# Row sums on one core: a body with its own semaphores behind an empty tile context, and no barrier at the end

## The chip, the cores and the metric

The kernel runs on one core of a Trainium2 chip. A core has five engines with instruction streams of their own: PE (TensorE, not used here), DVE (VectorE), ACT (ScalarE), POOL (GpSimd) and SP (SyncE, which issues transfers), and 16 DMA engines that work off the transfers. Engines and transfers order themselves by semaphores only. The metric is the device time of one execution in microseconds (us), as the median of several executions. Lower is better.

## The reference

```python
x = np.random.randn(32, 512, 1024).astype(np.float32)   # batch, seq, dim

def reference(x):
    return np.sum(x, axis=-1).astype(np.float32)
```

16384 rows of 1024 float32 are each added up to one number: 67.1 MB are read and 64 KB written.

## The kernel before

The rows are laid over the 128 partitions in two blocks. In the first block, 14336 rows, every partition has 112 rows of its own, in the second, 2048 rows, 16. A buffer (`xt`) holds 16 rows of every partition, 8 MB, and there are three of them (`bufs=3`, line 36).

**Loads.** SP issues all loads, in one queue. The loop of lines 84 to 99 runs over the seven buffers of the first block; each is loaded by two transfers, the even and the odd partitions (line 93). For the first buffer a small transfer with one row of every partition comes ahead of the two. A buffer can be loaded anew only when its sums are done. The second block comes in five pieces: 9, 4 and 2 rows into a buffer (line 107), and its last row in two parts of 544 and 480 columns into `tail` (line 110). Lines 145 to 164 move the first three loads to the start of the program, ahead of the barrier that the program begins with (its instructions are at line 178 of the profile).

**Sums.** DVE adds up whole buffers with one `tensor_reduce` each (line 47). Of the seventh buffer ACT takes seven rows (line 55, an `activation` with an accumulator, one row at a time). When the first block is done, ACT issues the store of its results in three transfers, the early stores (line 116). Of the pieces of 9 and 4 rows DVE takes 4 and 2, ACT 5 and 2; of the piece of 2 rows DVE takes the first, with an operation that adds the two halves of a row pairwise and accumulates (`pairs_dve`, line 67), and ACT the second. The last row is two pairwise sums on DVE: the first leaves its partial sum in a column of `tail`, and the second reads it back among its own inputs. Line 128 is a copy of two columns of `tail` between the two; nothing reads what it writes.

**Order.** The body is traced in a tile context, which gives each engine's instructions in program order and works out the semaphores: an increment behind an operation that another waits for, and waits attached to instructions, or in instructions of their own where there are several. Transfers use eight semaphores in turn, so that a ninth waits for the first. Line 132 puts SP's wait for ACT's last row in front of the last store (line 133).

**The end.** `tc.close()` and `tc.compile()` (lines 140 and 141) end the context: SP waits for every transfer, all engines meet in a barrier, POOL clears the context's semaphores, and all engines meet in a second barrier. In the profile these instructions stand at line 141.

Of the kernel before, what the change touches and what calls it, by code (L numbers as in the profile page):

```python
# [1 line left out]

# [4 lines left out]

F32 = mybir.dt.float32
ADD = mybir.AluOpType.add
COPY = mybir.ActivationFunctionType.Copy  # L10
X = mybir.AxisListType.X

BLOCKS = (112, 16)
G = 16
ACT_ROWS = 7
CUT = 544
EARLY = 3


@with_exitstack  # L20
def row_sums(
    ctx: ExitStack,
    tc: tile.TileContext,
    x: bass.AP,
    out: bass.AP,
):
    nc = tc.nc
    P = nc.NUM_PARTITIONS

    x_flat = x.flatten_outer_dims()  # L30
    R, D = x_flat.shape
    C = R // P
    assert R % P == 0 and sum(BLOCKS) == C
    out_flat = out.rearrange("a (b c) -> (a b c)", c=1)

    xpool = ctx.enter_context(tc.tile_pool(name="x", bufs=3))
    rpool = ctx.enter_context(tc.tile_pool(name="res", bufs=1))


    tail = rpool.tile([P, D + 16], F32, name="tail")  # L40
    part = tail[:, CUT + 14 : CUT + 15]
    nc.vector.memset(tail[:, CUT + 15 : CUT + 16], 0.0)  # L42
    seen = rpool.tile([P, 2], F32, name="seen")
    pairs = [rpool.tile([P, D // 2], F32, name=f"pairs{i}") for i in range(3)]

    def rows_dve(xt, res, j, n, c):
        nc.vector.tensor_reduce(  # L47
            out=res[:, c : c + n],
            in_=xt[:, j * D : (j + n) * D].rearrange("p (j d) -> p j d", d=D),
            axis=X,  # L50
            op=ADD,
        )

    def sum_act(v, acc):
        return nc.scalar.activation(out=v, in_=v, func=COPY, accum_out=acc)  # L55

    by_act = []

    def rows_act(xt, res, j, n, c):
        for i in range(n):  # L60
            by_act.append(
                sum_act(xt[:, (j + i) * D : (j + i + 1) * D], res[:, c + i : c + i + 1])
            )

    def pairs_dve(v, a, b, acc, pairs):
        h = (a + b) // 2
        nc.vector.tensor_tensor_reduce(  # L67
            out=pairs[:, 0 : h - a], in0=v[:, a:h], in1=v[:, h:b], scale=1.0, scalar=0.0,
            op0=ADD, op1=ADD, accum_out=acc,
        )  # L70

    def block(r0, n):
        x_b = x_flat[r0 : r0 + P * n].rearrange("(p c) d -> p (c d)", p=P)
        out_b = out_flat[r0 : r0 + P * n].rearrange("(p c) -> p c", p=P)
        return x_b, out_b, rpool.tile([P, n], F32, name=f"res{r0}")

    full = C - G
    done = 0
    for b, n in enumerate(BLOCKS):
        x_b, out_b, res = block(done * P, n)  # L80
        final = b == len(BLOCKS) - 1
        whole = n - G if final else n
        c = 0
        while c < whole:
            m = min(G, whole - c)
            xt = xpool.tile([P, G * D], F32, tag="xt", name="xt")


            parts = [(q, 0, m) for q in (slice(0, P, 2), slice(1, P, 2))]
            if done + c == 0:  # L90
                parts = [(slice(0, P), 0, 1)] + [(q, 1, m) for q, i, k in parts]
            for q, i, k in parts:
                nc.sync.dma_start(  # L93
                    out=xt[q, i * D : k * D], in_=x_b[q, (c + i) * D : (c + k) * D]
                )
            a = ACT_ROWS if done + c + m == full else 0
            rows_dve(xt, res, 0, m - a, c)
            rows_act(xt, res, m - a, a, c + m - a)
            c += m
        if not final:  # L100
            out_a, res_a = out_b, res
        done += n

    xt = xpool.tile([P, G * D], F32, tag="xt", name="xt")
    cuts = [0, 9, 13, 15]
    for i, k in zip(cuts, cuts[1:]):
        nc.sync.dma_start(out=xt[:, i * D : k * D], in_=x_b[:, (c + i) * D : (c + k) * D])
    last = 15 * D
    for i, k, gap in ((0, CUT, 0), (CUT, D, 16)):
        nc.sync.dma_start(  # L110
            out=tail[:, i + gap : k + gap],
            in_=x_b[:, c * D + last + i : c * D + last + k],
        )

    for i, k in ((0, 104), (104, 116), (116, P)):
        nc.scalar.dma_start(out=out_a[i:k], in_=res_a[i:k])

    by_act.clear()
    for i, k in zip(cuts[:2], cuts[1:3]):
        h = (k - i) // 2  # L120
        rows_dve(xt, res, i, h, c + i)
        rows_act(xt, res, i + h, k - i - h, c + i + h)
    pairs_dve(xt, 13 * D, 14 * D, res[:, c + 13 : c + 14], pairs[2])
    rows_act(xt, res, 14, 1, c + 14)
    pairs_dve(tail, 0, CUT, part, pairs[0])


    nc.vector.tensor_copy(out=seen, in_=tail[:, CUT + 14 : CUT + 16])  # L128
    pairs_dve(tail, CUT + 14, D + 16, res[:, c + 15 : c + 16], pairs[1])


    tc.keep_in_program_order(nc.sync.keepalive_nop([nc.sync.lower_ap(res[:, c + 14 : c + 15])]))
    store = nc.sync.dma_start(out=out_b, in_=res)
    for i in by_act:
        tc.declare_no_dep(store.ins, i.ins, reason="the wait is in the nop before it")


def kernel(tc: tile.TileContext, x: bass.AP, out: bass.AP):
    row_sums(tc, x, out)
    tc.close()  # L140
    tc.compile()  # L141

    sp = mybir.EngineType.SP
    fn = tc.nc.m.functions[0]
    entry, body = None, None
    for blk in fn.blocks:
        ops = [i for i in blk.instructions if i.engine == sp]
        if entry is None:  # L150
            entry = blk
        elif any(i.opcode == "DMACopy" for i in ops):
            body = blk
            break
    code = list(body.instructions)
    loads = [i for i in code if i.engine == sp][:EARLY]
    for load in loads:
        assert load.opcode == "DMACopy" and not load.sync_info.on_wait
        code.remove(load)
    body.instructions = code  # L160
    code = list(entry.instructions)
    at = next(k for k, i in enumerate(code) if i.engine == sp and i.opcode == "Drain")
    code[at:at] = loads
    entry.instructions = code

# [1 line left out]
_INS = ['x']  # L167
_OUTS = [((32, 512), 'float32')]


# [23 lines left out]
```

## Time and profile before

| | us |
|---|---|
| time, median of 3 runs (161.99 to 162.24) | 162.09 |
| profiled execution: span, first to last instruction | 160.28 |
| profiled execution: first instruction to the last semaphore event behind the span | 162.19 |
| DVE busy | 121.5 (76%) |
| ACT busy | 17.1 (11%) |
| DMA, mean over the span | 419 GB/s |

The span is what the profile shows of one execution; behind it the trace records only semaphore events, for another 1.91 us. The page names engines with a q (SPq, DVEq) for instructions of the engine's sequencer, such as waits, drains and the issue of transfers. They don't count as busy. A transfer has two times: when it is issued, and when it has landed, which is when the last of the 16 increments of its semaphore comes.

### The profile page before, as it was taken

The page shows a single profiled execution, that of the slowest core. Times are in us where ns is not written, and L with a number is a line of the kernel's source. Part 1 is how long each engine was busy: PE and PEld are TensorE (multiplying, and loading weights), DVE is VectorE, ACT ScalarE, POOL GpSimd, SP SyncE. Part 2 cuts the span into 40 slices and gives each one's busy share as a digit, 9 for nine tenths or more (in the row PEclk, how much of TensorE's full clock was granted, in tenths as well). Part 3 has the DMA queues.
Part 4 walks back from the last instruction along what each step waited for, and adds up shares of the span by engine and source line. Part 5 has one row for each costly group of instructions (what it writes and reads, how often), then busy time and mean ns, then how long its engine had stood idle before and what let it go on. Part 6 is the DMA issues. An engine that isn't in the chain of part 4 may idle for free.

```text
span 160.3 us, 138 instructions
## 1 busy us (share of the span) xinstructions
DVE 121.5 (76%) x17; ACT 17.1 (11%) x31; POOL 0.2 (0%) x4
## 2 busy tenths in 40 slices
DVE  0000059997699968999499994999949999599884
ACT  0000000000000000000000000000000000596694
POOL 0000000000000000000000000000000000000000
DMA  9979996996996996996997998979969969998991
GB/s 376 491 337 399 491 523 262 523 523 262 523 507 278 523 491 294 523 491 294 523 474 311 523 409 376 523 343 442 523 278 507 523 262 523 432 432 370 402 407 66
DMA packets 2293, 67.18 MB, mean 419 GB/s; under 512 B 629, under 2 KB 757, under 8 KB 1013
## 3 DMA queue, kind: packets, MB, share of 16 engines
q1 hardware_dynamic: 2128, 67.12, 97.4%
q10 hardware_dynamic: 165, 0.06, 0.1%
HBM read 67.11 MB, written 0.07 MB: 419 GB/s over the span
## 4 chain that ended last, share of the span: by engine, by line
DMA 73%; DVE 23%; another core or an unknown queue 1%; SPq 1%; issue 0%; DVEq 0%
DMA xt<-in_x_dram 73%; DVE res L47 21%; DVE pairs L67 1%; SPq L93 1%; DVE seen L128 0%; DVEq L47 0%; DVE tail L67 0%; DVE res L67 0%; DVEq L141 0%
## 5 line engine op out<-in xcount | busy, mean ns | idle before, releaser
L47 DVE TENSOR_REDUCE res<-xt 128x16 f32<-128x16384 f32 (+3 forms) x9 | 119.8, 13309 | 34.0 <-DMA xt<-in_x_dram 34.0
L55 ACT ACT_TABLE_LOAD x1 | 1.3, 1283 | 138.2 <-DMA xt<-in_x_dram 138.2
L55 ACT ACTIVATE xt<-xt 128x1024 f32<-128x1024 f32 x15 | 15.6, 1043 | 2.6 <-DMA out_dram<-res 2.6
L55 ACT ACTIVATION_READ_ACCUMULATOR xt<-xt 128x1 f32 x15 | 2.8, 187 | 0.0
L42 DVE MEMSET tail<- 128x1 f32 x1 | 0.1, 59 | 2.3 <-PEq L178 2.3
L67 DVE CUSTOM_DVE_ANT_0 pairs<-tail 128x272 f32<-128x272 f32 (+1 forms) x2 | 0.9, 426 | 0.0
L67 DVE CUSTOM_DVE_ANT_0 pairs<-xt 128x512 f32<-128x512 f32 x1 | 0.7, 692 | 0.2 <-DMA xt<-in_x_dram 0.2
L128 DVE COPY seen<-tail 128x2 f32<-128x2 f32 x1 | 0.2, 170 | 0.0
L67 DVE DVE_READ_ACCUMULATOR2_ANT res<- 128x1 f32 x2 | 0.2, 82 | 0.0
L178 POOL MEMSET const-bfloat16-1.0<- 128x1 bf16 x1 | 0.1, 102 | 0.0
L178 POOL MEMSET const-uint8-127<- 128x1 uint8 x1 | 0.1, 101 | 0.0
L178 POOL MEMSET const-float32-0.0<- 128x1 f32 x1 | 0.1, 99 | 0.2 <-issue 0.2
L178 POOL MEMSET const-float32-1.0<- 128x1 f32 x1 | 0.1, 98 | 0.0
L67 DVE DVE_READ_ACCUMULATOR2_ANT tail<- 128x1 f32 x1 | 0.1, 83 | 0.0
## 6 DMA issues: line engine op xcount, KB each, us to landing
xt<-in_x_dram SPq DMA_DIRECT2D x2, 3840.0 KB
xt<-in_x_dram SPq DMA_DIRECT2D x1, 4608.0 KB, 32.3
xt<-in_x_dram SPq DMA_DIRECT2D x1, 2048.0 KB, 36.8
xt<-in_x_dram SPq DMA_DIRECT2D x1, 1024.0 KB, 37.7
xt<-in_x_dram SPq DMA_DIRECT2D x1, 512.0 KB
tail<-in_x_dram SPq DMA_DIRECT2D x1, 272.0 KB, 28.6
tail<-in_x_dram SPq DMA_DIRECT2D x1, 240.0 KB, 19.5
xt<-in_x_dram SPq DMA_DIRECT2D x12, 38.5
```

What stands on the lines that cost most here:

```text
L42: nc.vector.memset(tail[:, CUT + 15 : CUT + 16], 0.0)
L47: nc.vector.tensor_reduce(out=res[:, c : c + n], in_=xt[:, j * D : (j + n) * D].rearrange("p (j d) -> p j d", d=D), axis=X, op=ADD,)
L55: return nc.scalar.activation(out=v, in_=v, func=COPY, accum_out=acc)
L67: nc.vector.tensor_tensor_reduce(out=pairs[:, 0 : h - a], in0=v[:, a:h], in1=v[:, h:b], scale=1.0, scalar=0.0, op0=ADD, op1=ADD, accum_out ...
L93: nc.sync.dma_start(out=xt[q, i * D : k * D], in_=x_b[q, (c + i) * D : (c + k) * D])
L128: nc.vector.tensor_copy(out=seen, in_=tail[:, CUT + 14 : CUT + 16])
L178: nc = _bacc.Bacc("TRN2", target_bir_lowering=False, num_devices=1)
```

## The change

The body is no longer traced in the tile context. The context is closed and compiled while it is empty, and the body is written behind it with waits and increments by hand. The three buffers, `tail` and the results are allocated directly. These are the edits:

- Each buffer has one semaphore for both halves (32 per round), each piece one of its own; DVE and ACT count their operations in `vec` and `act`.
- SP waits for a buffer's sum (`vec`) ahead of its next load and for nothing else; the waits for old transfers are gone, and the last five loads follow each other.
- The copy at line 128 is gone; the second sum of the last row waits for DVE's own count instead.
- In front of the last store SP waits for `vec` and for `act`.
- At the end SP waits for the early stores, clears all semaphores but one, and waits for the last store. No engine meets another.
- The first three loads are moved to the start of the program as before.

```diff
-    nc.vector.tensor_copy(out=seen, in_=tail[:, CUT + 14 : CUT + 16])
-    pairs_dve(tail, CUT + 14, D + 16, res[:, c + 15 : c + 16], pairs[1])
-    tc.keep_in_program_order(nc.sync.keepalive_nop([nc.sync.lower_ap(res[:, c + 14 : c + 15])]))
-    store = nc.sync.dma_start(out=out_b, in_=res)
-    for i in by_act:
-        tc.declare_no_dep(store.ins, i.ins, reason="the wait is in the nop before it")
...
+    nc.vector.wait_ge(sems["first"], 16)
+    for b in range(n_bufs):
+        a = ACT_ROWS if b == n_bufs - 1 else 0
+        nc.vector.wait_ge(slots[b % BUFS], 32 * (b // BUFS + 1))
+        rows_dve(xt[b % BUFS], 0, G - a, res_a, b * G)
+        freed[b] = count["vec"]
+        if a:
+            nc.scalar.wait_ge(slots[b % BUFS], 32 * (b // BUFS + 1))
+            rows_act(xt[b % BUFS], G - a, a, res_a, b * G + G - a)
+    body_vec, body_act = count["vec"], count["act"]
+    nc.scalar.wait_ge(vec, body_vec)
+    nc.scalar.wait_ge(act, body_act)
     for i, k in ((0, 104), (104, 116), (116, P)):
-        nc.scalar.dma_start(out=out_a[i:k], in_=res_a[i:k])
+        nc.scalar.dma_start(out=out_a[i:k], in_=res_a[i:k]).then_inc(sems["early_store"], 16)
+    for k in range(2):
+        i, j = CUTS[k], CUTS[k + 1]
+        h = (j - i) // 2
+        nc.vector.wait_ge(sems[f"piece{k}"], 16)
+        rows_dve(last, i, h, res_z, i)
+        nc.scalar.wait_ge(sems[f"piece{k}"], 16)
+        rows_act(last, i + h, j - i - h, res_z, i + h)
+    nc.scalar.wait_ge(sems["piece2"], 16)
+    rows_act(last, 14, 1, res_z, 14)
+    nc.vector.wait_ge(sems["piece2"], 16)
+    pairs_dve(last, 13 * D, 14 * D, res_z[:, 13:14], pairs[2])
+    nc.vector.wait_ge(sems["tail0"], 16)
+    pairs_dve(tail, 0, CUT, tail[:, CUT + 14 : CUT + 15], pairs[0])
+    nc.vector.wait_ge(sems["tail1"], 16)
+    nc.vector.wait_ge(vec, count["vec"])
+    pairs_dve(tail, CUT + 14, D + 16, res_z[:, 15:16], pairs[1])
...
+    for b, dst, src, s in loads:
+        if b >= BUFS:
+            nc.sync.wait_ge(vec, freed[b - BUFS])
+        nc.sync.dma_start(out=dst, in_=src).then_inc(s, 16)
+    nc.sync.wait_ge(vec, count["vec"])
+    nc.sync.wait_ge(act, count["act"])
+    nc.sync.dma_start(out=out_z, in_=res_z[:, :]).then_inc(sems["store"], 16)
+    nc.sync.wait_ge(sems["early_store"], 48)
+    nc.sync.sem_clear(range(numbers[0], sems["store"].num))
+    nc.sync.wait_ge(sems["store"], 16).then_inc(sems["store"], -16)
...
 def tile_reduce_tiled_1024_kernel(tc: tile.TileContext, x: bass.AP, out: bass.AP):
-    row_sums(tc, x, out)
     tc.close()
     tc.compile()
+    nc = tc.nc
+    row_sums(nc, x, out)
```

## The prediction

> **What bounds the kernel now.** I read the page from the top (span, queues, chain), then the timeline of the last 12 us, then the instructions of line 141, which is the closing of the tile context, and last the trace's record of semaphore events, which gives times to the nanosecond. The page:
>
> ```profile
> span 160.3 us, 138 instructions
> ...
> q1 hardware_dynamic: 2128, 67.12, 97.4%
> ...
> ## 4 chain that ended last, share of the span: by engine, by line
> DMA 73%; DVE 23%; another core or an unknown queue 1%; SPq 1%; issue 0%; DVEq 0%
> ```
>
> Queue q1 carries the loads and keeps the 16 DMA engines busy for 97.4% of the span. The chain of work is DMA for 73%; its DVE part is the wait for a buffer to come free, at times when another buffer is already under way. So the loads run without a gap until the last one lands, at 157.56 by the semaphore record, and everything ahead of that is hidden behind them. What can change the time is what comes after. The timeline from there on:
>
> ```profile
> 156.35 0.69 DVE L67 CUSTOM_DVE_ANT_0 pairs<-xt 128x512 f32<-128x512 f32 x1 [0.20 <-DMA xt<-in_x_dram]
> ...
> 157.02 0.44 DVE L67 CUSTOM_DVE_ANT_0 pairs<-tail 128x272 f32<-128x272 f32 x1
> 157.39 0.08 DVE L67 DVE_READ_ACCUMULATOR2_ANT tail<- 128x1 f32 x1
> 157.51 0.17 DVE L128 COPY seen<-tail 128x2 f32<-128x2 f32 x1
> 157.59 0.41 DVE L67 CUSTOM_DVE_ANT_0 pairs<-tail 128x241 f32<-128x241 f32 x1
> 157.70 0.19 ACT L55 ACTIVATION_READ_ACCUMULATOR xt<-xt 128x1 f32 x1
> 157.92 0.08 DVE L67 DVE_READ_ACCUMULATOR2_ANT res<- 128x1 f32 x1
> 158.04 0.35 SPq L133 DMA_DIRECT2D out_dram<-res  x1
> ```
>
> Columns: start, duration, engine, line. The last sum starts 0.02 us after the last load has landed, and the store is issued 0.03 us after that sum is out (its semaphore event is at 158.016). The store lands 1.42 us later, at 159.46. SP sees it at 159.478 and is through that wait at 159.506. Then line 141:
>
> ```profile
> L141 SPq EVENT_SEMAPHORE  x7: 17/28/28, 158.4 to 160.2; - x7
> L141 POOLq EVENT_SEMAPHORE  x4: 17/17/17, 159.6 to 160.2; - x4
> L141 POOLq DRAIN  x3: 34/41/77, 2.2 to 160.0; - x3
> L141 SPq DRAIN  x3: 7/7/7, 159.5 to 159.8; - x3
> ...
> L141 PEldq EVENT_SEMAPHORE  x2: 51/51/51, 159.8 to 160.2; - x2
> L141 POOLq EVENT_SEMAPHORE_RANGE_CLEAR  x1: 95/95/95, 159.9 to 159.9; - x1
> ```
>
> After the count come the durations in ns (least, median, most) and the first and last start. Behind the store stand a barrier of all engines, POOL's clearing of the semaphores and a second barrier; PE's wait ends the span at 160.284.
>
> **What lies around the span.** The semaphore record goes on: nine events on one semaphore from 160.519 to 161.044, a row of clearings to 161.607, and nine more events on the same semaphore from 161.831 to 162.189. Counted from the first instruction this execution took 162.19; the runs shown have 161.99 to 162.24, median 162.09. So I take the time as span (160.28) plus this closing (1.91), work out differences on it, and subtract them from the median.
>
> **The change, part by part.**
>
> *The barrier at the end goes.* SP's wait for the store now ends the program: what stood from 159.506 to 160.284 falls away, **-0.78 us**. SP's other new work at the end (the wait for the early stores, one clearing) stands between the end of the store's issue at 158.39 and its landing at 159.46, 1.07 us; the early stores landed by 149.53, and POOL's clearing took 0.095. Without that cover it would cost some 0.15.
>
> *The empty context's closing moves to the front.* Drains, two barriers and POOL's step now stand between SP's third and fourth load, about 160.28 - 159.54 = 0.74 us, so the fourth load starts near 3.0 instead of 2.23. The three loads ahead of the barrier hold the whole first buffer, whose second half lands at 21.88: some 19 us of cover. Uncovered, it would cost its 0.74. DVE's memset is later too, and its first sum starts at 22.0. **0.**
>
> *Waits of their own, in the body.* A wait attached to an instruction lets it start 0.023 us after the event (event 157.484, copy 157.507; the same for the four rows at 153.863). A wait standing alone in front lets it start after 0.092 (landing 41.227, sum 41.319). So a wait that comes off its instruction costs 0.07. A buffer's sum already paid the 0.092 before; two halves on one semaphore change nothing there. Queued behind SP's wait for a free buffer are only more loads. When buffer 0 is refilled at 39.25, buffer 1 lands at 41.23 and buffer 2 at 60.61: 21 us of work is queued, so the refills and the vanished waits of SP for old transfers are worth **0**. The last five loads, issued from 116.65 to 138.03 before, now go out together from 116.7, behind the same data in the same queue: the last landing stays.
>
> *The same waits, in the tail.* The last sum now has two: for the load, standing alone (+0.07), and for DVE's own count, attached (nothing) or alone (about +0.06, as SP's waits follow each other at 158.442, 158.496, 158.563, 158.622). DVE +0.07 to +0.13. The removed copy gives nothing: the last sum started 0.024 after its load landed, so the load held it, not the copy. SP had one attached wait, 0.026 from event to store; with the waits for DVE and ACT in front the store starts 0.05 to 0.12 later. ACT gets one wait more in front of the early stores (+0.06), and it then ends at 157.96, still ahead of DVE's 158.1; its new increments are free, since rows with and without one have the same pitch of 1.040. Whether a wait stays alone the trace of before can't show, so the ends are 0 (all attached) and +0.27. I take a middle value, **+0.17**, since the nearest rows, waits for a landing ahead of a sum, stand alone.
>
> *The closing after the program.* Before, the engines came into it together: the third event came 0.205 after the second (0.038 in the later nine), so one engine was late. Now PE, POOL, ACT and DVE are through by 158.2, over 1 us before SP, and only SP's own arrival counts. From an engine's last instruction to its event I have two rows: 160.284 to 160.519, 0.235, and, if the late one was POOL (last instruction over at 160.197), 160.758, 0.56. From the order of the clearings that follow I infer that SP is the fifth event, at 160.826 before, from which the end was 1.363. With 0.24 the closing takes 1.60 instead of 1.91, **-0.30**. The ends: 0.18 (the shortest step at the start, from an engine's event to its first instruction) makes -0.36; 0.56 with SP first in the order (1.50 from its event on) makes +0.16.
>
> The Trainium skill speaks against the change here: "Runtime: NRT & Kernel Launch", section "The ~15µs preamble/postamble breakdown", says the runtime adds a barrier over all engines after the kernel itself, about 1.5 us. Were that paid in full after SP, against the 0.76 from 160.284 to 161.044 here, an estimate by that page makes the sum +0.13, or 162.2. The row decides for me.
>
> Sum: -0.78 + 0.17 - 0.30 = -0.91; 162.19 becomes 161.28, and on the median 162.09 becomes **161.2**.
>
> **Rivals.** (A) As summed: 161.2. (B) The closing keeps its 1.91, since SP's own step into it is as long as the late one's: -0.78 + 0.17 = -0.61, 161.5. For it speaks the 0.56 row; against it the 0.235, and that SP's waits are among the shortest (17 to 28 ns). (C) The change does not do what it says: a barrier stays behind SP's last wait, from the compile or from the launch. Then -0.78 and -0.30 fall out and +0.17 stays, 162.25. Against it: line 141 is the only source of barriers at the end, and line 178 has its own at the start alone. (D) Slower: five loads queued at once at 116.7, where nine are then outstanding and SP's waits for old transfers kept it at eight, fill the queue; issuing blocks, and ACT's early stores at 147.95 with it. ACT's last eight rows then slip one for one. ACT has 0.12 us of slack to DVE's end, so it decides from 0.12 + 0.91 = about 1.0 us of hold, and shows as slower from 1.35. Held until the four-row load lands at 153.84, the stores come 5.9 later: 161.2 + 5.9 - 0.12 = 167.0. Against it: at the start seven loads of three whole buffers go out back to back at 0.6 us each, unblocked, and the bytes outstanding are never more than three buffers.
>
> **How the numbers follow.** This kernel's measurement can tell about 0.2%, 0.32 us: faster is below 161.77, slower above 162.41. A 0.53, B 0.31, C 0.10, D 0.06. The bounds of the unknown terms: -0.78 + 0 - 0.36 = -1.14, 160.95, and -0.78 + 0.27 + 0.16 = -0.35, 161.74; with 0.1 for the spread of the runs the range is 160.85 to 161.85. That holds A and B, and leaves out C and D, 0.16. Of A and B 0.01 lies within 0.2%: faster 0.83, same 0.11, slower 0.06.
>
> **What would show it.** In the changed profile: no instruction later than SP's wait for the store, and the span near 159.7; line 141's instructions all before 4 us; the fourth load near 3.0; the last load still landing near 157.6; the store issued 158.05 to 158.3; nine events that start before SP's end and close about 1.6 us after it. Wrong it would be with a last landing moved by over 0.3, with barrier instructions behind the store, with ACT's early stores later than 148.1, or with the closing at 1.9.

## The result

The changed kernel takes 160.87 us (median of 5 runs, 160.84 to 161.00) against 162.06 (median of 5, 161.96 to 162.24): a ratio of 0.9926, with a 95% interval of 0.9914 to 0.9939. That is 1.19 us, or 0.7%, and far outside the 0.2% that a measurement can tell. The forecast was 161.2, with 160.85 to 161.85 as its range; the time lies at the very edge of it, 0.02 us inside.

The page of the changed kernel shows the body as it was and a shorter span:

```profile
span 159.5 us, 116 instructions
...
q1 hardware_dynamic: 2128, 67.12, 97.8%
...
## 4 chain that ended last, share of the span: by engine, by line
DMA 73%; DVE 23%; SPq 1%; issue 0%; DVEq 0%
```

The same 67.12 MB in the same 2128 packets, and a queue that is busy throughout; the last load lands at 157.517, where it was 157.563, and e12 below shows that this difference means nothing. Up to there nothing is won. The timeline of the end (start, duration, engine, line):

```profile
156.42 0.69 DVE L73 CUSTOM_DVE_ANT_0 pairs<-xt 128x512 f32<-128x512 f32 x1 [0.32 <-DMA xt<-in_x_dram]
...
157.04 0.44 DVE L73 CUSTOM_DVE_ANT_0 pairs<-tail 128x272 f32<-128x272 f32 x1
157.40 0.08 DVE L73 DVE_READ_ACCUMULATOR2_ANT tail<- 128x1 f32 x1
157.46 0.18 ACT L66 ACTIVATION_READ_ACCUMULATOR xt<-xt 128x1 f32 x1
157.63 0.41 DVE L73 CUSTOM_DVE_ANT_0 pairs<-tail 128x241 f32<-128x241 f32 x1
157.97 0.08 DVE L73 DVE_READ_ACCUMULATOR2_ANT res_z<- 128x1 f32 x1
158.08 0.35 SPq L141 DMA_DIRECT2D out_dram<-res_z  x1
```

Between 157.40 and 157.63 stands no copy any more; the last sum starts at 157.63 instead of 157.59 and the store goes out at 158.08 instead of 158.04. So up to the store the changed kernel is not ahead, but 0.035 us behind. What follows the store is one clearing and one wait on SP, lines 145 and 146:

```profile
L145 SPq EVENT_SEMAPHORE_RANGE_CLEAR  x1: 52/52/52, 158.5 to 158.5; - x1
```

```profile
L146 SPq EVENT_SEMAPHORE  x1: 17/17/17, 159.5 to 159.5; - x1
```

The store lands at 159.496, SP's wait ends at 159.529, and with it the span. The context's closing, line 151 now, has gone to the front; the last two figures of a line's times are the first and last start:

```profile
L151 POOLq EVENT_SEMAPHORE  x4: 17/17/17, 2.4 to 2.8; - x4
L151 SPq DRAIN  x3: 7/7/7, 2.2 to 2.6; - x3
...
L151 PEldq EVENT_SEMAPHORE  x2: 51/51/51, 2.5 to 2.8; - x2
```

Behind the span the semaphore record shows the same closing as before, nine events, clearings, nine events. The first nine, in us:

| event | 1 | 2 | 3 | 4 | 5 | 6 | 7 | 8 | 9 | end of the closing |
|---|---|---|---|---|---|---|---|---|---|---|
| before, span ends at 160.284 | 160.519 | 160.553 | 160.758 | 160.802 | 160.826 | 160.924 | 160.963 | 160.997 | 161.044 | 162.189 |
| after, span ends at 159.529 | 3.108 | 157.764 | 157.802 | 158.202 | 159.672 | 159.715 | 159.753 | 159.787 | 159.834 | 160.982 |

The changed kernel shows what the order is: the first event comes at 3.1, when PE is through; the second just after ACT's last instruction (157.647), the fourth after DVE's (158.050), the fifth after SP's (159.529). So PE, ACT, POOL, DVE, SP, and back. Only from the fifth event on does the closing lie behind the span, and from the end of the span to its last event it takes 1.453 us instead of 1.905.

Both executions together: 162.189 to 160.982 is 1.207. Of this 0.790 is the stretch from the store's landing to the end of the span (0.823 before, 0.033 after), 0.452 the closing, and -0.035 the later store.

### The profile page after: what moved, and what is told of

Read it like the earlier page. It is cut to its first block, busy times and chain, and to the rows that moved or that the text cites. A ratio compares the mean times of both kernels' runs of the same rounds, so it can differ in the third digit from the quotient of the medians.

```text
span 159.5 us, 116 instructions
## 1 busy us (share of the span) xinstructions
DVE 121.3 (76%) x16; ACT 17.1 (11%) x31; POOL 0.2 (0%) x4
## 3 DMA queue, kind: packets, MB, share of 16 engines
q1 hardware_dynamic: 2128, 67.12, 97.8%
## 4 chain that ended last, share of the span: by engine, by line
DMA 73%; DVE 23%; SPq 1%; issue 0%; DVEq 0%
DMA xt<-in_x_dram 73%; DVE res_a L55 22%; SPq L138 1%; DVE pairs L73 1%; DVEq L131 0%; DVE tail L73 0%; DVE res_z L73 0%
## 5 line engine op out<-in xcount | busy, mean ns | idle before, releaser
L55 DVE TENSOR_REDUCE res_a<-xt 128x16 f32<-128x16384 f32 (+1 forms) x7 | 113.1, 16153 | 31.7 <-DMA xt<-in_x_dram 31.7
L55 DVE TENSOR_REDUCE res_z<-xt 128x4 f32<-128x4096 f32 (+1 forms) x2 | 6.7, 3353 | 1.6 <-DMA xt<-in_x_dram 1.6
```

What stands on the lines that cost most here:

```text
L55: nc.vector.tensor_reduce(out=res[:, c : c + n], in_=t[:, j * D : (j + n) * D].rearrange("p (j d) -> p j d", d=D), axis=X, op=ADD,).then_i ...
```

## The experiments

All kernels below start from the changed kernel unless it is said otherwise. Times are medians. What is called the closing is the time from the end of the span to the last event of the semaphore record; an engine's step is the time from the end of its last instruction to its own event among the first nine. Each kernel has one profiled execution. In the six that end on SP alone (the changed kernel, e5, e6, e7, e8, e12) the closing is 1.45 to 1.46 us, in the four that end with a barrier (the kernel before, e1, e2, e11) 1.90 to 1.91.

### The old end put back: e1

```diff
-    nc.sync.sem_clear(range(numbers[0], sems["store"].num))
-    nc.sync.wait_ge(sems["store"], 16).then_inc(sems["store"], -16)
+    nc.sync.wait_ge(sems["store"], 16)
+    nc.all_engine_barrier()
+    nc.gpsimd.sem_clear(range(numbers[0], sems["store"].num + 1))
+    nc.all_engine_barrier()
```

> The changed kernel with the old end put back by hand: behind SP's wait for the last store a barrier of all engines, POOL's clearing of the semaphores, a second barrier; the body is untouched. Theory (the whole gain sits at the end: 0.79 us of barriers and 0.45 us of the closing after the span): both come back, span 160.3 and time 162.1. Rival (the hand-written waits made the body faster, or the closing is shorter because the context was empty): at least part of the gain stays, time 161.2 to 161.7.

162.01 us over 10 runs, against 162.10 of the kernel before on the same chip: ratio 0.9986, 0.9968 to 1.0005. From the store's landing (159.518) to the end of the span (160.196) 0.68 us, closing 1.903. The whole gain is gone. So the body with its own waits is worth nothing that can be told, and the rival falls.

### One barrier: e2

```diff
     nc.sync.wait_ge(sems["store"], 16).then_inc(sems["store"], -16)
+    nc.all_engine_barrier()
```

> The changed kernel with one barrier of all engines behind SP's last wait, nothing else. It tells the two terms apart. Theory (the closing gets shorter because the other engines are already there when SP comes): one barrier costs its own 0.33 us in the span, as those at the front of the changed kernel do, and the whole 0.45 of the closing is lost with it, time 161.65. Rival (the closing's length goes with what is cleared and not with who comes when): only the 0.33, time 161.2.

161.66 us. The waits of SP by line, with the total, the number and the longest in us:

```profile
...
SPq L146 <- SPq L146: 1.0, 1, 1.0
SPq L152 <- PEq L152: 0.5, 2, 0.3
SPq L141 <- DVE res_z L73: 0.3, 1, 0.3
SPq L191 <- PEq L191: 0.2, 1, 0.2
SPq L147 <- PEq L147: 0.2, 1, 0.2
```

Line 147 is the barrier added: SP waits 0.2 us in it, and the span is 0.28 longer than the store's landing and SP's 0.033 make it. The closing is 1.904 again. So the two terms are apart: a barrier costs its own 0.28, and having any barrier at the end costs 0.45 more in the closing, because it lets all engines come into the closing at once. Rival (C) of the prediction, which had 162.25 with a barrier left, put too much on it: with one barrier 0.44 us of the gain against the kernel before beside it (162.10) stays.

### Another engine ends the program: e3, e4, e9, e10

```diff
-    nc.sync.wait_ge(sems["store"], 16).then_inc(sems["store"], -16)
+    nc.tensor.wait_ge(sems["store"], 16).then_inc(sems["store"], -16)
```

and the same with gpsimd, scalar and vector.

> SP's wait for the last store is made PE's; SP ends after the clearing. Theory (the closing goes PE, ACT, POOL, DVE, SP and back, and counts from the last engine's arrival): PE needs 0.235 us for its step into it, as before the change, and all four steps up to SP (0.14) come after it: closing 1.73 instead of 1.45, PE's wait is 0.03 longer, time 161.15 to 161.2. Rival (the closing counts from the last arrival whoever it is): time 160.9.

> The same with POOL as the engine that waits for the last store. Theory: POOL was the late one before the change, 0.56 us from its last instruction to its event, then two steps up to SP: closing 1.99, time 161.4. If POOL's step is as short as SP's 0.14 after a mere wait, then 160.95, and the late engine of before was late because of POOL's clearing and drains.

> SP's wait for the last store is made ACT's. Theory (the order is PE, ACT, POOL, DVE, SP and back; the closing counts from the last engine's own step): ACT's step was 0.117 in the changed kernel, three steps up to SP take 0.106 and from SP's event to the end 1.36: closing 1.58, time 161.0. Rival (steps belong to the place in the order, not to the engine): SP, at the far end, is the best place, and each place nearer the start costs a hop more, ACT between POOL's 1.99 and PE's 1.78.

> SP's wait for the last store is made DVE's. Theory: DVE's step was 0.152, one hop of 0.024 to SP and 1.36 from there: closing 1.54, time 160.95. Rival as for ACT: closing between SP's 1.45 and POOL's 1.99, about 1.7.

| the last wait is on | time, us | step | closing |
|---|---|---|---|
| SP (changed kernel) | 160.87 | 0.143 | 1.453 |
| DVE | 160.99 | 0.182 | 1.569 |
| ACT | 161.06 | 0.149 | 1.616 |
| PE | 161.30 | 0.279 | 1.782 |
| POOL | 161.47 | 0.562 | 1.992 |

The times of the first two rows overlap in their runs (160.92 to 161.38 on DVE, 160.84 to 161.00 on SP); it is the closings that tell them apart. In the kernel that ends on POOL the last wait is an instruction of 17 ns like SP's own:

```profile
L146 POOLq EVENT_SEMAPHORE  x1: 17/17/17, 159.4 to 159.4; - x1
```

POOL's event follows 0.562 us later, exactly its step of before the change (0.561). So POOL came late then not because of its clearing and drains, but because its step into the closing is that long. That explains the jump between the second and third event: in a kernel that ends with a barrier POOL's step lies bare, and in the changed kernel POOL has made it by 157.8. The closings of POOL, ACT and DVE came within 0.04 of what the order and the steps gave, PE's within 0.06, since its step was 0.279 and not 0.235. The rival, that it is only the place in the order that counts, falls: POOL is third and the slowest, and ACT, the second, doesn't lie between PE's 1.782 and POOL's 1.992 but at 1.616.

### The copy put back: e5

```diff
+    seen = sbuf("seen", 2)
...
+    nc.vector.wait_ge(vec, count["vec"])
+    nc.vector.tensor_copy(out=seen[:, :], in_=tail[:, CUT + 14 : CUT + 16]).then_inc(vec, 1)
+    count["vec"] += 1
     nc.vector.wait_ge(sems["tail1"], 16)
-    nc.vector.wait_ge(vec, count["vec"])
     pairs_dve(tail, CUT + 14, D + 16, res_z[:, 15:16], pairs[1])
```

> The changed kernel with the small copy of before put back in front of the last sum, which waits for the partial sum in place of the last sum. Theory: the last sum has one attached wait again, and starts 0.024 us after the last load or 0.08 after the copy's start, whichever is later; 0.03 less than in the changed kernel, where a wait standing alone costs 0.105 after the event: time 160.84, the same within what can be told. Rival (the copy cost its 0.17 on the path): time 161.0.

160.89 us (160.80 to 160.98). The timeline:

```profile
157.50 0.09 DVE L74 DVE_READ_ACCUMULATOR2_ANT tail<- 128x1 f32 x1
157.62 0.17 DVE L132 COPY seen<-tail 128x2 f32<-128x2 f32 x1
157.70 0.41 DVE L74 CUSTOM_DVE_ANT_0 pairs<-tail 128x241 f32<-128x241 f32 x1
```

The copy takes 0.17, but the next operation starts 0.08 after its start, so it holds the last sum for 0.08. Here it is the copy that held it: the load had landed at 157.623, 0.074 before the sum. In the kernel before the two limits fell together (copy at 157.507, load at 157.563, sum at 157.587), so its trace can't tell which of them held the sum; the prediction put it down to the load alone. The wait of its own that takes the copy's place in the changed kernel holds the sum for 0.13 (event 157.497, sum 157.630; the 0.105 of the expectation counts from the start of that wait, 157.525). The time is the same within the spread; that the copy cost 0.17 is refuted, and that the copy is the faster by 0.03 can't be told.

### The front: e6, e7, e11

Eight more barriers between the empty context's closing and the body (e7), one early load in place of three (e6), and the kernel before with one early load (e11):

```diff
     nc = tc.nc
+    for _ in range(8):
+        nc.all_engine_barrier()
     row_sums(nc, x, out)
```

```diff
-EARLY = 3
+EARLY = 1
```

> Eight more barriers of all engines between the empty context's closing and the body. Theory (cost nothing, since the three loads ahead hold 19 us of work): the fourth load is issued about 2.6 us later, at 5.5, and the time stays at 160.87. Rival (a barrier costs its length wherever it stands): time 163.5.

> Only the first load stays ahead of the barriers, so that the barriers at the front lose their cover. Theory: the first load's 0.5 MB keeps the queue busy for 1.2 us, the second load is issued at 2.88 us instead of 0.43, and the DMA engines run dry for about 1.2 us: time 162.1, of which 0.65 is what the empty context's closing adds. Rival (the front is hidden whatever stands there): time 160.9.

> The kernel before with one early load instead of three: the program's first barrier stands ahead of the second load, but no closing of an empty context. With one early load the changed kernel lost 1.4 to 1.8 us, of which the second load's issue explains 0.99 (1.42 instead of 0.43). Theory (the closing in front costs its own 0.65 where nothing covers it, and the rest is the first barrier's): second load issued near 0.77, time 162.1 + 0.35 to 0.8, 162.5 to 162.9, so 0.65 to 1 less lost than in the changed kernel. Rival (the loss comes from issuing the big loads late at all, and the closing adds nothing): the same 1.4 to 1.8, 163.5 to 163.9.

e7: 160.78 us (160.76 to 161.04). The fourth load is issued at 5.55 instead of 2.88, and the last lands at 157.62. The front is hidden, as the prediction had it.

e6 and e11 were to give the price without cover, and both came out dearer than the theory said: e6 162.63 (162.25 to 163.05; expected 162.1) and e11 164.28 (163.24 to 164.62; expected 162.5 to 162.9), where the kernel before took 162.20 and 162.10 beside them. So one early load costs the kernel before, with no closing in front, more than it costs the changed one. My theory, that the closing adds its length there, is refuted as far as these two go. The rival of equal losses, 163.5 to 163.9, is neither shown nor excluded: its range lies inside the spread of e11's four runs. One premise was off besides: in e6 the second load goes out at 1.42 and not at 2.88, since with one load ahead of them the barriers are through at 1.41 instead of 2.87. What the trace shows is where the time goes. The landing of the first big load, in us, with its issue and the first, the fifteenth and the last of its 16 increments:

| | issued | 1st | 15th | 16th | from 1st to 16th |
|---|---|---|---|---|---|
| changed kernel | 0.43 | 12.04 | 12.56 | 12.81 | 0.77 |
| e7 | 0.42 | 12.15 | 12.59 | 12.65 | 0.50 |
| e6 | 1.42 | 12.94 | 13.70 | 13.99 | 1.05 |
| e11 | 0.78 | 12.39 | 13.11 | 15.38 | 2.98 |

In e11 fifteen parts of the load land by 13.11 and the last 2.27 us later; one of the packets of 60 KB that this load is made of takes 2.27 too (median in the trace). One of the 16 parts has fallen behind by about one packet's time at the start, and never makes it up: four loads later the increments are still 2.9 apart, in the last load 2.6, and that load lands at 160.12 instead of 157.5. In e6 all 16 are late by 0.9 to 1.2, and their spread of 1.05 stays as well. I read it so that each DMA engine has a fixed share of every load, and that the slowest one ends the kernel; the trace doesn't name the engines. The packets show where the two losses begin. The first 16 of 60 KB start at 2.63 to 3.40 in the changed kernel and take 2.27 each. In e11 fifteen start at 2.73 to 3.34 and one only at 4.99. In e6 they start at 2.95 to 4.13, 0.24 later in the median, and take 3.02 in the median: most of e6's delay is that these first packets are slower. The issue of the loads in e11 shows a stall: from the start of the first to the end of the seventh it is 5.71 us instead of 4.62, and one of them takes 1.70 alone, and the first sum starts at 24.58 instead of 22.00:

```profile
0.00 5.71 SPq L93 DMA_DIRECT2D xt<-in_x_dram  x7
...
24.58 17.22 DVE L47 TENSOR_REDUCE res<-xt 128x16 f32<-128x16384 f32 x1 [23.67 <-DMA xt<-in_x_dram]
```

Why one part starts late in e11, and why the first packets of e6 are slower, when none of this shows in the traces whose big loads go out at 0.43, I have not settled. So the price of the front without its cover stays open; that it costs nothing with it is shown.

### The last loads held, and the changed kernel again: e8, e12

```diff
+        if s is sems["piece2"]:
+            nc.sync.wait_ge(slots[2], 64)
+        if s is sems["tail0"]:
+            nc.sync.wait_ge(slots[0], 96)
         nc.sync.dma_start(out=dst, in_=src).then_inc(s, 16)
```

> The last loads are held back again as before the change: the third of the last five waits for the sixth buffer's landing (118.6 us), the fourth and fifth for the seventh's (138.0). Theory: the queue always has work, the last landing stays at 157.5, time 160.87. Rival (issuing the last five together is what moved the last landing from 157.56 to 157.52): 0.05 more, at most 160.95.

> The changed kernel once more, beside the next runs. Theory: the last landing of one and the same body was anywhere from 157.43 to 157.64 in the runs so far, so the time repeats to about 0.1 us: 160.8 to 161.0, closing 1.45. Rival (the 0.05 by which the last load landed earlier than before the change belongs to the change): it lands by 157.52 again.

e8: 160.94 us (160.78 to 160.95), the last loads issued at 118.57, 137.86 and 138.23, the last landing 157.59. e12, without any edit: 160.87 (160.73 to 161.02), the last landing 157.63, the closing 1.452. So the last landing of the same body wanders by some 0.3 us from run to run (157.43 to 157.70 over those above that load as the changed kernel does), and neither the order of the last loads nor the 0.05 by which the changed kernel's first profile was earlier means anything.

## Why the prediction was right

**Direction, place and mechanism held.** The gain is all at the end, e1 takes it back, and the likeliest case, (A), is the one that came. That the time fell into the range is in part luck: two terms were mis-sized by 0.15 and 0.135 us, both to the same side, and the 1.19 won is more than the 1.14 that the sum made with every term at its best. Only the 0.1 added for the spread of the runs took in 160.87.

**The barrier, -0.78.** Measured 0.790, from the store's landing to the end of the span.

**The closing, -0.30.** The mechanism held: only SP's arrival counts, and SP is the fifth of the order, as inferred. The size was off: 0.452. I took 0.24 for SP's step, from the only engine whose step could be seen alone, PE; SP's is 0.143, less than the 0.18 that I had as the low end. The way back from SP also was 0.05 shorter, since DVE's event follows SP's by 0.043 instead of 0.098. The rest of the closing, 1.27 from there on, is as before.

**The waits in the tail, +0.17.** This is the other term that was mis-sized: the store went out 0.035 later. The prediction had 0.07 to 0.13 for DVE and 0.05 to 0.12 for SP if the waits stand alone, and took a middle value (the two upper ends make 0.25, not its 0.27; nothing hangs on it). SP's part is nothing: the compiled program has the wait for ACT standing alone in front, at 157.672, long before DVE is done, and the one that comes last, for DVE, attached to the store, which starts 0.016 after the event (0.026 before):

```profile
L140 SPq EVENT_SEMAPHORE  x1: 17/17/17, 157.7 to 157.7; - x1
```

DVE's part comes from the wait for its own count, the one that stands alone on DVE in the tail:

```profile
L131 DVEq EVENT_SEMAPHORE  x1: 21/21/21, 157.5 to 157.5; - x1
```

In all eleven traces with this wait the last sum starts 0.132 or 0.133 after the event, also where its load had landed 0.189 before (e7), so the wait holds it and not the load. With the copy in its place the sum starts 0.10 after the event (0.103 before the change, 0.101 in e5), or 0.024 behind its load where that comes later. By this measure the wait costs 0.030 in the changed kernel's first profile (157.630 instead of 157.600) and 0.016 in e12 (157.670 instead of 157.654, with the load at 157.630), where the prediction had 0.07 at the least for a wait standing alone: it left out that the copy held the sum too. The waits that I took to stand alone because a buffer's sum had one before are attached now: the second buffer's sum starts 0.023 after its landing instead of 0.092. That is hidden by the loads.

**The front, 0, and the body, 0.** Shown by e7, e1 and e8. The fourth load was issued at 2.88, where I had 3.0. What it would cost uncovered I had as its 0.74; the runs don't support that figure, and I have no other.

**The rivals.** (B) the closing keeps its 1.91: refuted by 1.453, and by e1 and e2, in which it is 1.90 because a barrier is there. (C) a barrier stays: there is none. (D) the last five loads block the queue: they took 0.34 to 0.44 us each, back to back from 116.55, and ACT's early stores went out at 147.79, earlier than before.

**The skill's figure.** The 1.5 us of the Trainium skill for the runtime's barrier ("Runtime: NRT & Kernel Launch", section "The ~15µs preamble/postamble breakdown") is not what this case shows: from the end of the span to the ninth event are 0.305 us when SP comes last and the others are there, 0.76 when all come at once. The measurement decides.

## What to carry to other kernels

An end where one engine waits for the last store is worth more than the barrier it saves (here 0.45 us on top of 0.79): engines that are done early make their way into the closing while the last one still works, and a barrier at the end takes that away from all of them, above all from the one with the longest way (here POOL, 0.56 us). Let the engine with the shortest way be the last (here SP, 0.143). Extra barriers at the front cost nothing while transfers already issued cover them: eight more, with a whole buffer on its way, left the time as it was, but with a single small load ahead of them the time rose (e6, e11). In a kernel whose transfers run without a gap a gain is to be looked for behind the last of them, and there each wait is to be asked whether it comes last or is long satisfied.

## What the runs showed that I had not expected

- The closing of the program depends on which engine is last: 1.45 us with SP, 1.57 with DVE, 1.62 with ACT, 1.78 with PE, 1.99 with POOL, and 1.90 with all at once.
- One of the 16 parts of the loads that falls behind at the start keeps its lag to the end: in e11 one packet's 2.27 us, in an execution that took 2.5 us more than the kernel before.
- ACT's table load moved from 138.18 to 2.89 us, since in the changed kernel nothing stands in front of it but the barriers. ACT's first sum then starts at 138.01 instead of 139.48, which wins nothing: its early stores wait for DVE's nine-row sum and go out 0.15 earlier, mostly because that sum starts 0.10 earlier:

```profile
2.89 1.28 ACT L66 ACT_TABLE_LOAD   x1 [2.89 <-PEq L151]
```
